# Mixture of experts in a two-layer backbone: 64 slots per expert and unsplit float32 weights in two column halves, instead of 128 slots per group and split weights

## The chip, the cores and the metric

The kernel runs on one core of one Trainium2 chip. The metric is the device time of one execution in microseconds (us), and the kernel before is given by the median of three runs.

## What is computed

The program is a two-layer backbone over 256 latent tokens (with a prefix of 256 context tokens) of 1024 features, all in float32. Layer 0 is an RWKV-7 time mixer, layer 1 a short gated convolution; a mixture of 16 experts follows each of them, and a last norm ends it. The change touches the mixture alone. Of the reference it is this part (d is 1024, EXPERT_DIM 512):

```python
def _moe(h, router_w, router_b, w_gate, w_up, w_down):
    s = sigmoid(hf @ router_w)                         # 256 tokens x 16 experts
    sel = (s + router_b).reshape(-1, 4, 4)             # 4 groups of 4 experts
    group_score = sum(top_k(sel, 2)[0], axis=-1)
    g_idx = argmax(group_score)                        # one group for each token
    experts = g_idx * 4 + top_k(sel[g_idx], 2)         # two experts of this group
    gate = s[experts] / sum(s[experts])
    for e in range(16):
        he = silu(hf @ w_gate[e]) * (hf @ w_up[e])
        out = out + combine[:, e:e + 1] * (he @ w_down[e])
```

Each token takes two experts, so 256 tokens make 512 pairs of a token and an expert, 32 for an expert on average. With the inputs of this reference the fullest group has 84 tokens. In layer 0 no expert has more than 62. In layer 1 one expert, number 15, has 68, and all others have at most 64.

## The kernel before

In both mixtures each expert reads 6 MB of float32 weights: two tables of 1024 x 512 (gate and up) and one of 512 x 1024 (down). SyncE (SP) loads them in pieces of [128, 2048], 1 MB each, in the order of their use, which the generator `sources` (L1045) writes out; `wpiece` (L149) puts each into the next buffer of a ring of 8 (two of the kernel, six of the phase by `extra_ring`, NRING = 6).

A float32 table is not multiplied as it is. ScalarE (ACT) rounds each half piece to the shorter type that the program calls float32r (`wh`, L1078), and VectorE (DVE) subtracts that from the original (`wl`, L1081). The activations are split the same way, and `mm3` (L134) makes each product of three matmuls, high by high, high by low, low by high. `wnext` (L1084) hands out the split parts and `ahead` (L1066) keeps two parts ahead of their use.

The experts of a group share its tokens. `route_groups` (L1341) finds each token's group and its place among the group's tokens. `gather` (L1472) builds a one-hot matrix with 128 slots for each group (`onehot`, L1438) and multiplies the normed tokens with it, for two groups at once: `xe` holds them feature-major. A token that did not choose an expert goes through it all the same and gets the gate weight zero. `route_experts` (L1378) makes the gate weights.

The loop over the experts (L1595) is staggered, and the order of the instructions is the order in which it is written: the gate product of expert e (`half_up`, 8 blocks of 128 features x 3 matmuls of 512 columns), the turn of expert e - 1 (`turn`, `hetp`), the up product of e, and the down product of e - 1 (`down`, 24 matmuls of 512 columns). That makes 72 matmuls of 512 columns for an expert. The down products of the four experts of a group add up in PSUM (`y`), and once per group `scatter` (L1464, 16 matmuls of 256 columns) brings the sum from slots back to tokens. A new group's gate weights come from `gates` (L1450, `gps`).

If a group has more than 128 tokens, `rest` (L1548) computes what is left over. Its body is long (16 experts with weights read again) and stands under one branch for each layer, `tc.If(over > P)`, behind the last expert's turn. With these inputs the branch is never entered. Towards the end of a mixer, two calls `self.ahead(4)` have four parts of the next mixture's weights split beforehand, and the convolution's first weights are split in the same way while the last experts still run. Modulation that is needed late (`fill`, L1091) is computed in the routing, with weights that the caller loads at that point of the program.

## Time and profile before

| | us |
|---|---|
| median of three runs | 1435.24 |
| lowest and highest | 1433.29, 1442.48 |
| profiled execution, span from the first to the last instruction | 1432.6 |
| RWKV mixer, with its output product and the routing of layer 0 | 0 to 680.5 |
| experts of layer 0 | 680.5 to 985.6 |
| convolution mixer and routing of layer 1 | 985.6 to 1119.6 |
| experts of layer 1 | 1119.6 to 1421.0 |
| final norm | 1421.0 to 1432.6 |

The profile is one execution, taken by the hardware's profiler, and its span is the only time that it gives; the stages are cut in the same trace, where the first product of each begins. It is told in the names of the engines: PE is TensorE's matmuls, PEld its weight loads, SP the engine that issues the weights' DMAs. In a timeline the first number is the start in the span, the second the length of a row, and matmuls that follow one another overlap in it, so the cost of one is read from the distance of two starts. The granted clock is a share of full speed.

### The profile page before, as it was taken

To read this page: it belongs to the slowest core of one execution; us is meant where nothing else is said; L and a number is where in the kernel's file an instruction comes from. 1 tells how busy PE (TensorE), PEld (TensorE's weight loads), DVE (VectorE), ACT (ScalarE), POOL (GpSimd) and SP (SyncE) were. 2 spreads that over 40 slices of the span, in tenths; PEclk is the share of its full clock that TensorE was granted. 3 is DMA by queue.
4 is the path that set the end of the run, shared out by engine and by line. 5 is a ranking of instruction groups with operands and counts; after the bars stand their busy time and mean duration, and the time that the engine had idled before them with its cause. 6 is when DMAs were issued, how large, how long until landed. Compare 5 with 4: busy or idle time off the path is not lost. (4 is left out here: it accounts for less than half of the span.)

```text
span 1432.6 us, 23636 instructions
## 1 busy us (share of the span) xinstructions
PE 1289.7 (90%) x8848; PEld 1098.9 (77%) x8848; DVE 1183.9 (83%) x2139; ACT 936.5 (65%) x1499; POOL 235.2 (16%) x245
## 2 busy tenths in 40 slices
PE   2898797998888888998999999997988999999996
PEld 2688696777777777887778787876988778887875
DVE  5869888999989988767888888886685888898985
ACT  4675644676666676445777777765445678777765
POOL 3213525222222312001000000003233000000001
PEclk8899998999999999999999999998999899999998
DMA  9456443223314201386798999986545599999980
GB/s 366 148 170 215 148 141 101 95 91 115 109 32 152 73 25 67 132 319 241 280 348 316 339 349 339 346 322 243 173 154 192 193 354 329 332 344 342 346 292 31
DMA packets 64637, 311.75 MB, mean 218 GB/s; under 512 B 14464, under 2 KB 23040, under 8 KB 29696
## 3 DMA queue, kind: packets, MB, share of 16 engines
q1 hardware_dynamic: 60192, 303.59, 59.2%
q10 hardware_dynamic: 4320, 6.54, 1.3%
q8 instruction: 73, 1.20, 0.3%
q14 instruction: 52, 0.43, 0.1%
HBM read 301.72 MB, written 8.39 MB: 216 GB/s over the span
## 5 line engine op out<-in xcount | busy, mean ns | idle before, releaser
L1081 DVE TENSOR_TENSOR wl<-w,wh 128x1024 fp32r<-128x1024 f32 x411 | 497.6, 1224 | 77.4 <-ACT wh L1078 74.1
L1078 ACT CAST wh<-w 128x1024 fp32r<-128x1024 f32 x424 | 442.0, 1052 | 160.1 <-PE wup L139 69.9
L137 PE MATMUL wup<-wh,xe 128*128 128x512 f32 x512 | 205.4, 401 | 4.3 <-ACT sgate L1602 4.0
L138 PE MATMUL wup<-wl,xe 128*128 128x512 f32 x512 | 202.9, 396 | 0.2
L139 PE MATMUL wup<-wh,xe 128*128 128x512 f32 x512 | 202.3, 395 | 0.0
L137 PEld LDWEIGHTS wup<-wh,xe 128*128 128x128 f32 x512 | 96.1, 188 | 31.6 <-ACT sgate L1602 9.1
L139 PEld LDWEIGHTS wup<-wh,xe 128*128 128x128 f32 x512 | 96.1, 188 | 23.3 <-DVE xe L132 0.3
L138 PEld LDWEIGHTS wup<-wl,xe 128*128 128x128 f32 x512 | 96.2, 188 | 23.1 <-DVE wl L1081 1.6
L137 PE MATMUL y<-wh,het 128*128 128x512 f32 x256 | 102.4, 400 | 8.4 <-PEq L1550 8.4
L138 PE MATMUL y<-wl,het 128*128 128x512 f32 x256 | 102.8, 402 | 0.0
L139 PE MATMUL y<-wh,het 128*128 128x512 f32 x256 | 102.4, 400 | 0.0
L813 DVE TENSOR_TENSOR lv<-a_l,t_l 128x126 f32<-128x126 f32 (+22 forms) x248 | 82.5, 333 | 3.3
L815 DVE TENSOR_TENSOR t_l<-t_l,lv 128x126 f32<-128x126 f32 (+22 forms) x248 | 78.7, 317 | 3.4
L879 PE MATMUL po<-v_bd,hk 128*64 128x128 f32 (+1 forms) x256 | 56.4, 303 | 21.2 <-ACT s_bd L890 8.1
L137 PEld LDWEIGHTS y<-wh,het 128*128 128x128 f32 x256 | 48.9, 191 | 20.6 <-issue 9.2
L879 PEld LDWEIGHTS po<-v_bd,hk 128*64 128x64 f32 (+1 forms) x256 | 31.8, 163 | 41.2 <-ACT s_bd L890 12.8
L1666 POOL TENSOR_SCALAR idrw<-cst 128x1024 f32<-128x1024 f32 x2 | 5.5, 2773 | 343.4 <-PE acc L1469 314.5
L890 ACT COPY s_bd<-po 64x64 f32<-64x64 f32 x112 | 22.6, 204 | 54.6 <-DVE s_bd L889 52.6
L139 PEld LDWEIGHTS y<-wh,het 128*128 128x128 f32 x256 | 48.9, 191 | 11.6
L138 PEld LDWEIGHTS y<-wl,het 128*128 128x128 f32 x256 | 48.9, 191 | 11.3
L138 PE MATMUL dps<-xl,wh 128*128 128x258 f32 x192 | 55.6, 290 | 1.9 <-DVE xl L1271 1.0
L137 PE MATMUL dps<-xh,wh 128*128 128x258 f32 x192 | 55.3, 288 | 1.0 <-ACT rt L1148 1.0
(426 smaller groups left out, 3074.0 us busy)
## 6 DMA issues: line engine op xcount, KB each, us to landing
w<-in_wg SPq DMA_DIRECT2D x64, 1024.0 KB, 5.2
w<-in_wu SPq DMA_DIRECT2D x64, 1024.0 KB, 5.6
w<-in_wd SPq DMA_DIRECT2D x64, 1024.0 KB, 6.0
w<-in_ada SPq DMA_DIRECT2D x46, 1024.0 KB, 6.6
w<-in_sc_in SPq DMA_DIRECT2D x12, 1024.0 KB, 5.5
w<-in_rk SPq DMA_DIRECT2D x8, 1024.0 KB, 5.8
w<-in_wv SPq DMA_DIRECT2D x4, 1024.0 KB, 6.2
w<-in_wo SPq DMA_DIRECT2D x4, 1024.0 KB, 10.5
```

Source lines behind the costliest of these rows:

```text
L137: mm(out, lhs[0], rhs[0], start=start, stop=False)
L138: mm(out, lhs[0], rhs[1], start=False, stop=False)
L139: mm(out, lhs[1], rhs[0], start=False, stop=stop)
L813: nc.vector.tensor_mul(u, a_l[:, kk:kk + 1, kk + 1:].broadcast_to([P, m, n]), t_l[:, 0:m, kk:kk + 1].broadcast_to([P, m, n]))
L815: nc.vector.tensor_sub(t_l[:, 0:m, kk + 1:], t_l[:, 0:m, kk + 1:], u)
L879: nc.tensor.matmul(po[d][i], q.hk[d][g][:, j], q.vbd[:, 4 * g + j], start=True, stop=i == 0)
L890: nc.scalar.copy(sn[64:, 64:], p[0:64, 64:])
L1078: self.nc.scalar.copy(h, w)
L1081: eng.tensor_sub(l, w, h.bitcast(F32))
L1666: nc.gpsimd.tensor_scalar_mul(self.idrw[:, :, :P], kern.k("ident").unsqueeze(1).broadcast_to([P, NB, P]), 1.0)
```

## The change

**Slots.** Every expert gets its own 64 slots (SL = 64). `route` picks the best two experts of every group first, then the group, and numbers the tokens of each expert; `onehot` makes eight matrices of 64 slots for four experts, and `gather` gathers four experts x 64 = 256 columns in one product. `scatter` runs once per expert, not once per group.

**Products.** The weights are used as they are, in float32, one matmul where there were three. Since an expert's activations have only 64 columns, they fill one half of TensorE's columns: the gate product goes to rows 0 to 63 of a PSUM tile and the up product to rows 64 to 127, one after the other in the program, and the two halves of the down product in the same way. The gate weight is applied when the down product leaves PSUM. The scatter takes rows 0 to 63 and 64 to 127 in matmuls of their own (16 of 256 columns).

**The queue of the weights.** Gate and up come in one table, `wgu`, so that an expert takes four pieces `wgu` and two `wd`, in this order and without the stagger. The ring has 2 + 9 = 11 buffers (NRING = 9), and the modulation's weights (`fill`) come through it as well, in the order of `sources`. `pump` issues a load as soon as a buffer is given back by `done`. The splitting stays for the two mixers' own weights, with three buffers instead of four (WSB = 3), which lie in pools of those phases. So `ahead(4)` at the mixers' ends is gone, and the convolution's first weights are split only when its pool is there.

**Overflow.** Experts with more than 64 tokens have a second set of 64 slots, under branches: for each expert from the third on one branch with the gate and up products (`more_up`) and one with the down product and the scatter, both with the weights that are still in the ring; they are given back when the branch is passed (`done(4)`, `done(2)`). The first two experts give their pieces back at once, and have one branch each, which would read the weights again. `over` holds one bit for each expert. `rest` remains for experts with more than 128 tokens. That makes 31 branches for each layer where there was one. With these inputs two of them are entered, those of expert 15 in layer 1.

```diff
-NRING = 6
+NRING = 9
-WSB = 4
+WSB = 3
+SL = 64
+EARLY = 2
...
         def experts(l):
-            for e in range(E + 1):
-                if e < E:
-                    yield from pieces(io["wg"][l, e], io["wu"][l, e])
-                if e:
-                    yield from pieces(io["wd"][l, e - 1])
+            for e in range(E):
+                yield from pieces(io["wgu"][l, e], io["wd"][l, e])
...
+    def pump(self):
+        while len(self.coming) + self.held < self.nring + self.nextra:
+            src = next(self.src, None)
+            if src is None:
+                return
+            self.coming.append(self.wpiece(src))
+
+    def take(self):
+        self.pump()
+        self.held += 1
+        return self.coming.pop(0)
+
+    def done(self, n):
+        self.held -= n
+        self.pump()
...
-            self.ahead(4)
             ro.block(NB - 1)
...
-            def half_up(i, xe):
-                sl = slice(i * P, i * P + P)
+            def gate_up(xe, j, piece, after=lambda k: None):
                 pt = ps.tile([P, 512], F32, tag="m", name="wup")
-                for hf in range(4):
-                    wh, wl = self.wnext(2)
-                    for k in range(2):
-                        kc = hf * 2 + k
-                        self.mm3(pt, (xe[0][:, kc, sl], xe[1][:, kc, sl]), (wh[:, k], wl[:, k]),
-                                 kc == 0, kc == NB - 1)
-                return pt
+                for kc in range(NB):
+                    w = piece(kc)
+                    for i in range(2):
+                        nc.tensor.matmul(pt[SL * i:SL * i + SL], xe[:, kc, j], w[:, 512 * i:512 * i + 512],
+                                         start=kc == 0, stop=kc == NB - 1)
+                    after(kc)
+                sg = pool.tile([SL, FE], F32, tag="sg", name="sgate")
+                nc.scalar.activation(sg, pt[:SL], AF.Silu)
+                nc.vector.tensor_mul(sg, sg, pt[SL:])
+                return sg
...
+            def scatter(yh, yl, st, first=False, last=False):
+                for q in range(4):
+                    for k, y in enumerate((yh, yl)):
+                        for i in range(2):
+                            r = slice(SL * i, SL * i + SL)
+                            nc.tensor.matmul(acc[4 * i + q], y[r, q * P:q * P + P], st[r],
...
+            def many(e):
+                return tc.If((over & (1 << e)) > 0)
+
+            def more_up(e, piece, gw, st, het):
+                g = onehot(e, 1, SL, "go")
+                xe = pool.tile([P, NB, 1, SL], F32, tag="xo", name="xo", bufs=1)
+                for _ in gather(g, 1, xe):
+                    pass
+                gates(g, 0, e, gw, st)
+                turn(gate_up(xe, 0, piece), het)
...
+            for e in range(E):
+                g, xe = gx[e // 4]
+                ws, early = [], e < EARLY
+                sg = gate_up(xe, e % 4, taken(ws), release)
+                gw, st = gate_tiles()
+                gates(g, e % 4, e, gw, st)
+                if out:
+                    scatter(*out)
...
+                if not early:
+                    with many(e):
+                        more_up(e, kept(ws), *og)
+                    self.done(4)
+                wd = []
+                out = (*down(turn(sg, hets()), taken(wd), gw, release), st)
...
+                with many(e):
+                    if early:
+                        more_up(e, again(io["wgu"][l, e]), *og)
+                    scatter(*down(og[2], again(io["wd"][l, e]) if early else kept(wd), og[0]), og[1])
+                if not early:
+                    self.done(2)
+            rest()
```

The scheduler may place instructions of neighbouring steps between one another, so the order in the program is read from the built kernels. On TensorE before, in the middle of a usual expert, the products of the next expert's up table (`wup`), a quarter of the next gather (`xeps`) and the down products (`y`) stand as triples without a break (the numbers in names are buffers):

```order
L137 MATMUL wup<-wh,xe_7452 128x512
L138 MATMUL wup<-wl,xe_7452 128x512
L139 MATMUL wup<-wh,xe_7453 128x512
L1485 MATMUL xeps<-g,h2t_6796 128x256 x2
L1485 MATMUL xeps<-g,h2t_6797 128x256 x2
L1485 MATMUL xeps<-g,h2t_6796 128x256 x2
L1485 MATMUL xeps<-g,h2t_6797 128x256 x2
L137 MATMUL y<-wh,het_8165 128x512
L138 MATMUL y<-wl,het_8165 128x512
L139 MATMUL y<-wh,het_8166 128x512
```

On TensorE after, a usual expert behind its first branch: its own turn, the down products, three products of the next expert, and the compare of the second branch, behind which its body stands (`heto` is the overflow's hidden features):

```order
L1555 MATMUL hetp<-cst,sgate 128x64 x4
L1543 MATMUL wup<-w,xe 64x512
L1568 MATMUL y<-w,het 64x512 x8
L1543 MATMUL wup<-w,xe 64x512 x2
L1696 REGISTER_ALU
L1696 COMPARE_AND_BRANCH
L1568 MATMUL y<-w,heto 64x512 x8
L1582 MATMUL acc_7463<-st,yh 128x256
L1582 MATMUL acc_7464<-st,yh 128x256
```

What moved: a triple has become one matmul of 64 rows, 24 for an expert instead of 72, and TensorE comes to a compare twice in each expert from the third on. On SP before, at the end of layer 0's experts, the loads follow one another, and the one branch stands behind all of the experts' weights:

```order
L158 DMA w<-in_wg 128x2048 x2
L158 DMA w<-in_wu 128x2048 x2
L158 DMA w<-in_wd 128x2048 x4
L1546 TENSOR_LOAD r_cnti
L1550 COMPARE_AND_BRANCH
L1550 UNCONDITIONAL_BRANCH x2
L158 DMA w<-in_sc_in 128x2048
```

On SP after, in the middle of the experts:

```order
L1688 UNCONDITIONAL_BRANCH x2
L161 DMA w<-in_wgu 128x2048 x2
L1696 REGISTER_ALU
L1696 COMPARE_AND_BRANCH
L1696 UNCONDITIONAL_BRANCH x2
L161 DMA w<-in_wgu 128x2048 x2
L161 DMA w<-in_wd 128x2048 x2
L1688 REGISTER_ALU
L1688 COMPARE_AND_BRANCH
```

What moved: the queue of the loads now goes past two branches for each expert, and the pieces are issued two and four at a time behind them.

## Rows read from the trace of the kernel before

**Rows 1.** The page: busy time of the engines.

```profile
PE 1289.7 (90%) x8848; PEld 1098.9 (77%) x8848; DVE 1183.9 (83%) x2139; ACT 936.5 (65%) x1499; POOL 235.2 (16%) x245
```

**Rows 2.** Costliest groups of instructions, from the page.

```profile
L1081 DVE TENSOR_TENSOR wl<-w,wh 128x1024 fp32r<-128x1024 f32 x411 | 497.6, 1224 | 77.4 <-ACT wh L1078 74.1
L1078 ACT CAST wh<-w 128x1024 fp32r<-128x1024 f32 x424 | 442.0, 1052 | 160.1 <-PE wup L139 69.9
```

**Rows 3.** Windows: us, busy PE, PEld, DVE, ACT, POOL, PEclk, DMA share, GB/s.

```profile
630.00:640.00 10.00, 9.81 (x116) 7.91 (x115) 7.11 (x20) 3.36 (x10) 0.61 (x1) 1.00 1.00 423
1160.00:1360.00 200.00, 198.34 (x907) 160.28 (x906) 176.74 (x165) 155.51 (x173) 0.00 (x0) 1.00 0.95 339
680.50:985.60 305.10, 296.34 (x1342) 238.32 (x1345) 260.61 (x247) 226.38 (x249) 0.00 (x0) 0.99 0.90 324
1119.60:1421.00 301.40, 296.03 (x1338) 238.04 (x1337) 258.23 (x245) 225.78 (x250) 0.00 (x0) 0.99 0.84 300
```

**Rows 4.** TensorE's timeline where the experts of layer 0 begin: start us, us.

```profile
680.82 0.39 PE L138 MATMUL wup<-wl,xe 128*128 128x512 f32 x1
681.05 0.40 PE L139 MATMUL wup<-wh,xe 128*128 128x512 f32 x1
```

**Rows 5.** TensorE's timeline before the routing: products of 32 columns of stationary.

```profile
661.11 0.65 PE L179 MATMUL fillps<-w,sc 128*32 128x128 f32 x16
661.68 0.76 PE L1684 MATMUL htps<-idrw,h 128*128 128x144 f32 x4
...
664.42 3.04 PE L179 MATMUL fillps<-w,sc 128*32 128x128 f32 x102
```

**Rows 6.** Groups by form, 560 to 1432 us: busy us, mean ns of one.

```profile
L1611 DVE SCALAR_TENSOR_TENSOR sgate<-sgate,gw,wup 128x512 f32<-128x512 f32 x32 | 23.7, 741 | 1.0 <-PE wup L139 1.0
L1602 ACT ACTIVATE sgate<-wup 128x512 f32<-128x512 f32 x32 | 19.1, 598 | 16.0 <-PE wup L139 16.0
...
L179 PE MATMUL fillps<-w,sc 128*32 128x128 f32 x256 | 8.6, 275 | 0.4 <-ACT rt L1148 0.4
```

**Rows 7.** TensorE's timeline, small products among the experts of layer 0.

```profile
686.19 0.38 PE L1454 MATMUL gps<-cst,g 128*128 128x128 f32 x2
...
687.03 0.50 PE L137 MATMUL wup<-wh,xe 128*128 128x512 f32 x1
...
771.78 0.60 PE L1517 MATMUL hetp<-cst,sgate 128*128 128x128 f32 x4
772.13 0.36 PE L1469 MATMUL acc<-st,yh 128*128 128x256 f32 x1
...
778.33 1.10 PE L1485 MATMUL xeps<-g,h2t 128*128 128x256 f32 x8
779.27 0.28 PE L1469 MATMUL acc<-st,yh 128*128 128x256 f32 x1
...
780.93 0.40 PE L137 MATMUL y<-wh,het 128*128 128x512 f32 x1
```

**Rows 8.** Instructions of the branch, line 1550: duration ns min/median/max.

```profile
L1550 PEldq COMPARE_BRANCH  x2: 3539/4778/6016, 968.5 to 1407.0; - x2
L1550 DVEq COMPARE_BRANCH  x2: 63/68/72, 968.9 to 1408.0; - x2
...
L1550 DVEq EVENT_SEMAPHORE  x2: 21/21/21, 969.5 to 1408.2; - x2
```

**Rows 9.** TensorE's timeline behind the branch, and at the convolution's start.

```profile
974.63 0.76 PE L137 MATMUL y<-wh,het 128*128 128x512 f32 x1 [5.68 <-PEq L1550]
...
986.54 0.39 PE L137 MATMUL dps<-xh,wh 128*128 128x258 f32 x1
```

**Rows 10.** VectorE's timeline in the routing of layer 0.

```profile
667.54 0.16 DVE L1334 TENSOR_REDUCE r_mg<-r_gs 128x2 f32<-128x8 f32 x1
...
667.73 0.17 DVE L1335 TENSOR_TENSOR r_gh<-r_gs,r_mg 128x8 f32<-128x8 f32 x1
```

**Rows 11.** ScalarE's timeline at the start of the convolution mixer.

```profile
992.38 1.99 ACT L1078 CAST wh<-w 128x1024 fp32r<-128x1024 f32 x2
```

More of the change, by code (lines that the diff above doesn't have):

```diff
@@ L1069, in ahead @@
             if not self.loaded:
[L1070 to L1073 removed]
+                t = self.take()
                 self.loaded += [t[:, :1024], t[:, 1024:]]
@@ L1513, in turn, with again, piece, taken @@
-            def turn(sg):
-                pt = ps.tile([P, 4, P], F32, tag="m", name="hetp")
+                    yield
+            def again(src):
+                def piece(k):
+                    w = pool.tile([P, 1024], F32, tag="wov", name="wov")
+                    nc.gpsimd.dma_start(w, src[:, k * 1024:k * 1024 + 1024])
+                    return w
+                return piece
+            def taken(ws):
+                def piece(k):
+                    if k % 2 == 0:
+                        ws.append(self.take())
+                    return ws[-1][:, k % 2 * 1024:k % 2 * 1024 + 1024]
+                return piece
@@ L1516, in turn @@
+            def turn(sg, het):
+                pt = ps.tile([P, 4, SL], F32, tag="m", name="hetp")
                 for k in range(4):
[L1517 to L1539 removed]
@@ new lines, in turn, with hets, down @@
+                    nc.tensor.transpose(pt[:, k], sg[:, k * P:k * P + P], self.k("ident")[:SL, :SL])
+                nc.scalar.copy(het, pt)
+                return het
+            def hets():
+                return pool.tile([P, 4, SL], F32, tag="het", name="het")
+            def down(het, piece, gw, after=lambda k: None):
+                y = psy.tile([P, 512], F32, tag="y", name="y")
+                for k in range(4):
+                    w = piece(k)
+                    for i in range(2):
+                        nc.tensor.matmul(y[SL * i:SL * i + SL], het[:, k], w[:, 512 * i:512 * i + 512],
+                                         start=k == 0, stop=k == 3)
+                    after(k)
+                yh = pool.tile([P, 512], F32R, tag="yh", name="yh")
+                yl = pool.tile([P, 512], F32R, tag="yl", name="yl")
+                nc.scalar.activation(yh, y, AF.Copy, scale=gw)
+                nc.vector.scalar_tensor_tensor(yl, y, gw, yh.bitcast(F32), op0=ALU.mult, op1=ALU.subtract)
+                return yh, yl
@@ new lines, in scatter @@
+            def scatter(yh, yl, st, first=False, last=False):
+                for q in range(4):
+                    for k, y in enumerate((yh, yl)):
+                        for i in range(2):
+                            r = slice(SL * i, SL * i + SL)
+                            nc.tensor.matmul(acc[4 * i + q], y[r, q * P:q * P + P], st[r],
+                                             start=first and q % 2 + k == 0, stop=last and k == 1,
+                                             skip_group_check=True)
@@ L1594, in moe @@
[L1594 to L1616 removed]
+                                nc.tensor.transpose(pt[:, k], sgs[t][:, k * P:k * P + P], self.k("ident"))
@@ new lines, in group @@
+            def group(e0, turns):
+                g = onehot(e0, 4, 0, "g")
+                xe = pool.tile([P, NB, 4, SL], F32, tag="xe", name="xe")
+                gx.append((g, xe))
+                yield from gather(g, 4, xe, 2, turns)
+            gx = []
+            for _ in group(0, (psy, ps)):
+                pass
+            cmb = self.weights(one, s, o)
+            ci = self.counts(one, o)
+            over, most = [nc.values_load(ci[0:1, i:i + 1], min_val=0, max_val=m,
+                                         skip_runtime_bounds_check_because=why)
+                          for i, (m, why) in enumerate((((1 << E) - 1, "one bit for each of the experts"),
+                                                        (T, "a count of the T tokens")))]
@@ L1619, in moe @@
                     out = None
-                if mid is not None:
-                    if e % 4 == 1:
-                        y = [psy.tile([P, 512], F32, tag="y", name="y") for _ in range(2)]
-                        yst = st
-                    out = down(het, y, e % 4 == 1, e % 4 == 0, yst if e == E else None)
-                    out = (*out, yst) if out[0] is not None else None
-                mid = nxt
-            scatter(*out, False, True, range(NB // 2, NB))
+                if e % 4 == 0 and e + 4 < E:
+                    nxt = group(e + 4, (psy, psy))
@@ new lines, in moe @@
+                if nxt and next(nxt, 0) == 0:
+                    nxt = None
+                og = (*gate_tiles("o"), pool.tile([P, 4, SL], F32, tag="heto", name="heto", bufs=1))
+                if not early:
[4 more added lines that the diff above has]
+                out = (*down(turn(sg, hets()), taken(wd), gw, release), st)
+                if e == 0:
+                    scatter(*out, first=True)
+                    out = None
```

378 lines of the change are left out of this document (167 added, 211 removed).

## The prediction, made before the changed kernel ran

> **What bounds the kernel now.** I read the page's busy times first: TensorE has 90% of the span and VectorE 83% [rows 1]. The second number comes from the splitting: 411 subtractions of 1.22 us make 497.6 us, and ScalarE's 424 roundings 442.0 us [rows 2]. That looks like two engines at the limit, so the windows must decide [rows 3]. The two stretches of the experts last 305.1 and 301.4 us, and TensorE is busy for 296.3 and 296.0 of them; in the 200 us window inside layer 1's stage it is busy for 198.3, VectorE for 176.7, ScalarE for 155.5. TensorE bounds the experts. The copies do not: they run at 339 GB/s there, though their engines show a share of 0.95, and the same queue moved 423 GB/s from 630 to 640 us, where it had a backlog. In the experts the products stand 0.23 us apart (681.05 - 680.82) [rows 4], so the 72 products of an expert take 72 x 0.233 = 16.8 of the 19.07 us that an expert has (305.1 / 16; in layer 1 301.4 / 16 = 18.84).
>
> So the question is what one expert costs TensorE after the change. I call it p.
>
> **The products.** An expert has 24 float32 products of 512 columns, each with 64 columns of stationary. The nearest thing in the trace is the modulation's `fillps`: unsplit float32, 128 columns moving, 32 columns of stationary, four quarters in turn. Its 64 products stand as 128 records, two for a product, 118 of them in [rows 5]. 102 of these take 3.04 us; less the 0.275 us that the last one lasts (mean in [rows 6]), 101 distances make 2.765 us, 27.4 ns each, and four quarters 109.5 ns. This is what one product of 256 columns of the shorter type takes (14 of them between 779.27 and 780.93, 0.119 each [rows 7]). I read two things there: a float32 record streams its columns twice, and the four quarters run abreast. A record of 512 columns then takes 4 x 109.5 = 438 ns, two halves abreast 219 ns each, and the expert's 48 records 10.5 us. If the halves ran one after the other it would be 21.0; I take 10.5, since quarters that did not overlap could not stand 27.4 ns apart. The matmuls of a pair that meet a new piece or another tile start alone: I add 0.4 (0 to 0.8).
>
> **The small products.** The gate weights (`gps`) come once per expert instead of once per four: 687.03 - 686.19 = 0.84 [rows 7]. The gather: eight `xeps` in 779.27 - 778.33 = 0.94, now eight per expert. The turn (`hetp`): 772.13 - 771.78 = 0.35. The scatter, 16 products of 256 columns for each expert: 16 x 0.119 = 1.9 one after another, 0.95 if the row halves run abreast. No row shows row halves; I take 1.2.
>
> **Changes between halves and whole.** In [rows 5] 16 records from 661.11 end their issue at 661.11 + 16 x 0.0274 = 661.55, and the next, whole product starts at 661.68: 0.13 lost. Five such changes in an expert make 0.6 (0 to 1.2). The Trainium skill ("TensorEngine Tiling (Array Packing)", Key Properties) says that changing the tiling mode drains TensorE; 0.13 is smaller than the 0.275 that a record lasts, so by a full drain it would be 5 x 0.275 = 1.4 and the sum 0.8 x 32 = 26 us higher, an estimate.
>
> **The branches.** From the third expert on, each has two. The row of before has only a branch over a very long body: TensorE's compare lasted 3.5 and 6.0 us [rows 8], and TensorE stood idle for 5.68 us in layer 0 [rows 9]. VectorE, over a body of the same branch but with fewer instructions, needed 0.07 us for the compare, and its next event came 0.6 and 0.2 us later. The new bodies are short on TensorE (some 56 products and 24). I take 0.5 for each branch, between VectorE's lower 0.2 and twice its upper 0.6, nearest to VectorE's rows; hence 1.0 for an expert. What is queued behind: `hetp`, whose activations have long been ready, and the next products. For the wait on `het` behind ScalarE's copy, under which only one product stands, I add 0.2 (0 to 0.6).
>
> p = 10.5 + 0.4 + 0.84 + 0.94 + 0.35 + 1.2 + 0.6 + 1.0 + 0.2 = 16.0 us. All upper ends make 18.9. The lower ends make less than the copies allow: six pieces of 1.049 MB at 423 GB/s [rows 3] are 14.9 us, which is the lower bound that I use. A ring of 11 pieces, with some given back late, should keep that backlog, so TensorE remains the bound, narrowly. What covers the loads is that backlog: SP's queue now goes past two branches for each expert, and a piece whose buffer is given back behind one may be asked for late. Without cover, one late piece would cost 1.049 / 423, 2.5 us. The splitting that goes, 12 roundings and 12 subtractions of half pieces for an expert, wins nothing by itself, since it lay beside TensorE.
>
> **The stages.** Layer 0: 16 x 16.0 = 256.0, plus the first expert's scatter, which cannot hide its copies (1.5), plus the branch over `rest`, still long (mean of 3.5 and 6.0, 4.8): 262.3, that is 42.8 less than 305.1. Layer 1 enters the two bodies of expert 15, the last one. Gather 32 x 0.119 = 3.8, `gps` 0.84, 32 records 7.0, turn 0.35, 16 records 3.5, scatter 1.2, and two chains through ScalarE and VectorE with nothing beside them, 1.3 each (by the activation and the product at the gates of before, 0.598 + 0.741 [rows 6]): 19.3. The stage is then 281.6, 19.8 less than 301.4.
>
> **The rest of the program.** The routing has 20 short VectorE steps ahead of the ranks where it had 10. A step takes 667.73 - 667.54 = 0.19 [rows 10], but in before other steps stood between them, so I take 1 us for each layer (0 to 3). The convolution's first weights are no longer split in advance. ScalarE's first cast in that mixer stands at 992.38 [rows 11], behind the activations, where TensorE had begun at 986.54 [rows 9]; with 1.05 and 1.22 for the first cast and subtraction [rows 2], TensorE could begin 8 us later. Part of it returns, as TensorE then finds parts waiting: 5 (0 to 8).
>
> Sum: -42.8 - 19.8 + 2 + 5 = -55.6. The profiled span of 1432.6 becomes 1377.0; the median of the runs is 2.6 above that span, so 1380 us. One microsecond of p is worth 32 us; the change gains nothing at p = 17.7.
>
> **The rivals.** *The copies set the pace.* If the small costs lie at their lower ends, p falls to 14.9: 1.1 x 32 = 35 less, 1345 us. For it: most of my small terms are bounds rather than rows. Against it: the pieces are given back in fours and twos behind branches, which costs backlog.
>
> *The gain is eaten on TensorE.* Branches at 1.2 us add 1.4 to p, 1425 us; the scatter's row halves one after another add 0.7 more, 1447. For it: no row shows either. Against it: VectorE's 0.2 to 0.6.
>
> *Every branch costs like the one of before.* This is the way to the slower side. There are 60 branches besides `rest`. At 3.5 us, the lower of the two that TensorE showed, they cost 60 x 3.0 = 180 more, 1560 us; at 6.0, 1710. It decides from 0.5 + 55.6 / 60 = 1.4 us per branch. For it: the only rows on TensorE. Against it: the body jumped there holds the products of 16 experts, the new ones a part of one. The Trainium skill ("Runtime: NRT & Kernel Launch", Instruction fetch mechanics) says that a taken branch whose target lies outside the current two pages of instructions must fetch them first; by it the new short jumps stay cheap, and only `rest` pays.
>
> *The halves do not run abreast.* Then p is 10.5 higher, 336 us, 1716. Against it stands [rows 5]; for it, only that those were quarters, of 32 columns each.
>
> **How the numbers follow.** A measurement of this kernel can tell about 1% from no change. Forecast (p from 15.3 to 17.2, 1358 to 1418): 0.57. Copies: 0.17. Gain eaten (1425 to 1447): 0.13. Branches dear: 0.09; halves in turn: 0.04. The first two are faster by over 1% (below 1421), 0.74; the third is within 1% for the most part, 0.13; the last two slower, 0.13. The range goes from below the copies' case, 1338, to the end of the third case, 1448.
>
> **What would show it.** Starts of `wup` records 0.22 us apart in the middle of an expert; a `MATMUL` group of 16 `acc` of 1.0 to 1.9 us; TensorE's compares at lines 1688 and 1696 under 0.6 us, except in expert 15 of layer 1; the rate of the copies near 390 GB/s in the experts; a gap of some 5 us at the start of the convolution. Starts 0.44 us apart, idle time of several microseconds put down to TensorE's queue at these two lines, or TensorE waiting for `w` in most experts would make the prediction wrong.

## The result: slower by 1.7%, and the profile after

The changed kernel takes 1460.5 us (median of five runs, 1459.43 to 1471.34) against 1438.8 us for the kernel before (five runs): a ratio of 1.0169, with an interval of 1.0142 to 1.0195. Forecast were 1380 us, with 1338 to 1448 as the range. The profiled execution is the longest of the five, 1471.34 us, with a span of 1469.3; a second profile has 1465.8, and its first stage of experts is the same to 0.1 us. This is where its time went, stage by stage, against the working of the prediction (each stage ends where TensorE begins the next):

| stage | before | foretold | after |
|---|---|---|---|
| mixer of layer 0, to the first `fillps` | 660.1 | 660.1 | 672.4 |
| routing of layer 0 | 20.4 | 21.4 | 22.6 |
| experts of layer 0 | 305.1 | 262.3 | 296.6 |
| convolution mixer | 116.4 | 121.4 | 120.9 |
| routing of layer 1 | 17.7 | 18.7 | 18.9 |
| experts of layer 1 | 301.4 | 281.6 | 324.6 |
| rest | 11.6 | 11.6 | 13.3 |

The span is 92.3 us over the 1377.0 of the working, and 34.3 + 43.0 of that lie in the two stages of the experts, 12.3 in the first mixer. The other rows are within 2 us. The page after, the busy times and the largest groups (to be held against [rows 1] and [rows 2]):

```profile
PE 1235.0 (84%) x8842; PEld 863.7 (59%) x8842; DVE 740.9 (50%) x1823; ACT 561.0 (38%) x1155; POOL 234.4 (16%) x245
...
L1543 PE MATMUL wup<-w,xe 128*64 128x512 f32 x1024 | 258.5, 617 | 4.1 <-PEq L1696 2.0
...
L1568 PE MATMUL y<-w,het 128*64 128x512 f32 x512 | 141.4, 690 | 11.2 <-ACT het L1556 11.2
L1574 DVE SCALAR_TENSOR_TENSOR yl<-y,gw,yh 128x512 fp32r<-128x512 f32 x33 | 24.8, 751 | 200.0 <-ACTq L1696 182.0
```

No engine is at its limit any more. VectorE has fallen from 83% to 50%, as the splitting went, and TensorE from 90% to 84%. The windows of the two stages (columns as in [rows 3]) say the same of the copies:

```profile
695.00:991.60 296.60, 247.53 (x1272) 107.26 (x1271) 35.40 (x77) 38.68 (x76) 0.00 (x0) 0.95 0.86 341
844.00:880.00 36.00, 30.46 (x150) 12.76 (x152) 3.22 (x7) 4.27 (x9) 0.00 (x0) 0.91 0.86 348
1131.40:1456.00 324.60, 276.73 (x1378) 120.42 (x1377) 38.95 (x87) 43.49 (x85) 0.00 (x0) 0.92 0.70 276
```

In layer 0's stage TensorE is idle for 296.6 - 247.5 = 49.1 us, 3.1 for each expert, where before it was idle for 8.8; the granted clock is 0.95; the copies run at 341 GB/s, far from 423. The instructions of the first branch of each expert are these:

```profile
L1688 PEldq COMPARE_BRANCH  x29: 77/325/422, 736.6 to 1439.8; - x29
...
L1688 DVEq COMPARE_BRANCH  x29: 47/56/63, 739.3 to 1439.0; - x29
```

The jump itself is cheap: 0.33 us on TensorE's queue, 0.06 on VectorE's, both in the median. What costs is seen in TensorE's largest waits of the stage (us in total, times, longest; L1688 is the first branch of an expert, L1696 the second, L1605 the one over `rest`):

```profile
PE hetp L1555 <- DVEq L1688: 21.1, 14, 1.6
PE acc L1582 <- ACTq L1696: 7.1, 9, 0.8
PE acc L1582 <- PEq L1605: 6.8, 1, 6.8
PE y L1568 <- ACT het L1556: 5.6, 12, 0.5
PE gps L1488 <- DVEq L1696: 4.4, 8, 0.6
```

How the first of them comes about is shown by all engines' timeline around one branch (start us, us, engine):

```profile
841.78 1.03 PE L1543 MATMUL wup<-w,xe 128*64 128x512 f32 x4
842.85 0.59 ACT L1547 ACTIVATE sgate<-wup 64x512 f32<-64x512 f32 x1 [3.03 <-PE wup L1543]
...
843.48 0.69 DVE L1548 TENSOR_TENSOR sgate<-sgate,wup 64x512 f32<-64x512 f32 x1 [3.07 <-ACTq L1688]
...
844.37 0.43 PE L1555 MATMUL hetp<-cst,sgate 64*128 64x64 f32 x4 [1.56 <-DVEq L1688]
844.84 0.37 ACT L1556 COPY het<-hetp 128x256 f32<-128x256 f32 x1 [1.40 <-PE hetp L1555]
...
845.26 1.07 PE L1568 MATMUL y<-w,het 128*64 128x512 f32 x2 [0.46 <-ACT het L1556]
```

TensorE's last `wup` ends at 842.8. Then ScalarE's activation (0.59) and VectorE's product (0.69) run one after the other with nothing beside them, the branch is passed on each engine in turn (the releasers are ACTq and DVEq of L1688, the queues' branch instructions), and TensorE starts its turn 1.56 us later and waits 0.46 more for the copy. The first pair of its down products then lasts 1.07 us where 0.64 is usual (the pair at 848.68, once the clock is back). TensorE's own timeline shows what that comes to, 16 records of each kind:

```profile
839.15 3.65 PE L1543 MATMUL wup<-w,xe 128*64 128x512 f32 x16
...
845.26 5.35 PE L1568 MATMUL y<-w,het 128*64 128x512 f32 x16 [0.46 <-ACT het L1556]
```

The same work takes 5.35 us behind the waits and 3.65 ahead of them. The granted clock of the stretch behind the waits (columns as above) is 0.51, the lower of its two levels (1.2 of 2.4 GHz), after 2.5 us in which TensorE did nothing but the turn:

```profile
845.26:848.68 3.42, 3.42 (x8) 0.96 (x10) 0.00 (x0) 0.00 (x0) 0.00 (x0) 0.51 0.99 417
```

### The profile page after: what moved, and what is told of

Read it like the earlier page. It is cut to its first block, busy times and chain, and to the rows that moved or that the text cites. A ratio compares the mean times of both kernels' runs of the same rounds, so it can differ in the third digit from the quotient of the medians.

```text
span 1469.3 us, 23339 instructions
## 1 busy us (share of the span) xinstructions
PE 1235.0 (84%) x8842; PEld 863.7 (59%) x8842; DVE 740.9 (50%) x1823; ACT 561.0 (38%) x1155; POOL 234.4 (16%) x245
## 5 line engine op out<-in xcount | busy, mean ns | idle before, releaser
L1543 PE MATMUL wup<-w,xe 128*64 128x512 f32 x1024 | 258.5, 617 | 4.1 <-PEq L1696 2.0
L1543 PEld LDWEIGHTS wup<-w,xe 128*64 128x64 f32 x1024 | 76.6, 139 | 126.5 <-issue 118.5
L1568 PE MATMUL y<-w,het 128*64 128x512 f32 x512 | 141.4, 690 | 11.2 <-ACT het L1556 11.2
L1574 DVE SCALAR_TENSOR_TENSOR yl<-y,gw,yh 128x512 fp32r<-128x512 f32 x33 | 24.8, 751 | 200.0 <-ACTq L1696 182.0
L1548 DVE TENSOR_TENSOR sgate<-sgate,wup 64x512 f32<-64x512 f32 x33 | 22.8, 690 | 192.0 <-ACT sgate L1547 100.5
L1547 ACT ACTIVATE sgate<-wup 64x512 f32<-64x512 f32 x33 | 19.5, 590 | 200.1 <-PE wup L1543 200.1
L1568 PEld LDWEIGHTS y<-w,het 128*64 128x64 f32 x512 | 44.7, 155 | 85.3 <-issue 68.4
L884 PE MATMUL po<-v_bd,hk 128*64 128x128 f32 (+1 forms) x256 | 56.6, 304 | 20.8 <-ACT s_bd L895 7.5
L1582 PE MATMUL acc<-st,yh 64*128 64x256 f32 x264 | 45.9, 314 | 26.6 <-ACTq L1696 14.2
L1102 ACT CAST wh<-w 128x1024 fp32r<-128x1024 f32 x40 | 41.6, 1046 | 48.3 <-PE dps L141 32.3
L1582 PEld LDWEIGHTS acc<-st,yh 64*128 64x128 f32 x264 | 29.8, 193 | 46.7 <-ACTq L1696 30.2
L142 PE MATMUL dps<-xh,wl 128*128 128x258 f32 x192 | 55.7, 290 | 0.6 <-POOL wl L1105 0.6
```

The source lines that it names most:

```text
L142: mm(out, lhs[1], rhs[0], start=False, stop=stop)
L884: nc.tensor.matmul(po[d][i], q.hk[d][g][:, j], q.vbd[:, 4 * g + j], start=True, stop=i == 0)
L1102: self.nc.scalar.copy(h, w)
L1543: nc.tensor.matmul(pt[SL * i:SL * i + SL], xe[:, kc, j], w[:, 512 * i:512 * i + 512], start=kc == 0, stop=kc == NB - 1)
L1548: nc.vector.tensor_mul(sg, sg, pt[SL:])
L1568: nc.tensor.matmul(y[SL * i:SL * i + SL], het[:, k], w[:, 512 * i:512 * i + 512], start=k == 0, stop=k == 3)
```

## The experiments

Theory A: the branches. An engine passes one only when it has finished all that stands ahead of it, and what uses a tile that the body could have touched waits for the other engines' passing too. Theory B: the lost stagger. In the kernel before, the turn of expert e - 1 stood behind a product of expert e, so the activation had time; now the activation that the turn needs comes from the product just ahead of it.

**Without branches (e1).** With no branch to keep them for, the pieces of all experts are given back at once.

```diff
-EARLY = 2
+EARLY = E
...
-                if not early:
-                    with many(e):
-                        more_up(e, kept(ws), *og)
-                    self.done(4)
...
-                with many(e):
-                    if early:
-                        more_up(e, again(io["wgu"][l, e]), *og)
-                    scatter(*down(og[2], again(io["wd"][l, e]) if early else kept(wd), og[0]), og[1])
-                if not early:
-                    self.done(2)
```

> The changed kernel without the 30 branches of each layer and their bodies; it leaves out the second 64 slots (4 tokens of expert 15 in layer 1). In the changed kernel's trace TensorE is idle for 49 and 48 us in the two stages, about 3 us per expert. Theory A (each branch is a point where an engine must have finished all that is ahead of it): idle falls to under 1 us per expert and the granted clock returns to 1.0, p from 18.3 to about 15.4; 2 x 16 x 2.9 = 93 less, and 20 less for the bodies of expert 15, from 1460 to about 1350 us. Theory B (the chain from the last gate and up product through ScalarE and VectorE to the turn is bare because the loop has lost its stagger): only the waits at line 1696 go, about 1.3 us per expert, 42 + 20 less, about 1400 us, and the wait ahead of hetp stays near 1.5 us.

Measured: 1372.37 us, ratio 0.9525 (0.9482 to 0.9567), between the two. Layer 0's stage:

```profile
694.80:958.40 263.60, 235.33 (x1272) 107.48 (x1271) 36.54 (x80) 38.22 (x76) 0.00 (x0) 0.99 0.98 382
```

That is 33.0 us shorter, so the stage's 30 branches cost 1.1 us each. Of the 33.0, 20.8 are idle time and 12.2 busy time, at a granted clock of 0.99 where it was 0.95; 3.8 of the idle time are the jump over `rest`, 3.0 here against 6.8, which the edit does not touch. That the pieces come back earlier has no large part in it: in the changed kernel's stage no wait of TensorE is put down to a load, and 0.5 us ahead of `wup` to nothing that the profile names. But 28 us of idle time stay, and most of it is the bare chain (waits of TensorE, 736 to 930 us; total, times, longest):

```profile
PE hetp L1555 <- DVE sgate L1548: 11.3, 8, 1.4
PE y L1568 <- ACT het L1556: 5.2, 10, 0.5
```

So both theories hold a part.

**One branch for each expert (e2).** Both bodies in one branch, behind the down products.

```diff
-                if not early:
-                    with many(e):
-                        more_up(e, kept(ws), *og)
-                    self.done(4)
...
                 with many(e):
-                    if early:
-                        more_up(e, again(io["wgu"][l, e]), *og)
+                    more_up(e, again(io["wgu"][l, e]) if early else kept(ws), *og)
                     scatter(*down(og[2], again(io["wd"][l, e]) if early else kept(wd), og[0]), og[1])
                 if not early:
-                    self.done(2)
+                    self.done(6)
```

> One branch for each expert instead of two, behind the down products, with gate and up, down and scatter in its body; all six pieces are kept until it is passed. Theory A: half of the joins go; with some 1.5 us each and the clock, 45 less, about 1415 us. Theory B: the chain ahead of hetp stays, within 10 us of 1460. If the ring of 11 is short with six pieces held, TensorE waits for w and the time is above 1460.

Measured: 1445.82 us, ratio 1.0053 (1.0030 to 1.0076): 15 less than the changed kernel, between the two expectations again. Layer 0's stage lasts 287.3 us, with 16 branches where there were 30. A removed branch saved (296.6 - 287.3) / 14 = 0.66 us, less than half of what theory A said. The wait ahead of the turn stayed without the branch, now put down to the product that it needs, and the wait at the remaining branch grew from 7.1 us to 11.0 (waits of TensorE in the stage):

```profile
PE hetp L1555 <- DVE sgate L1548: 13.4, 10, 1.4
PE acc L1582 <- ACTq L1692: 11.0, 14, 0.8
```

**The stagger back, the branches kept (e3).** The gate and up products of e + 1 stand ahead of the branch of e.

```diff
-                yield from pieces(io["wgu"][l, e], io["wd"][l, e])
+                if e < E:
+                    yield from pieces(io["wgu"][l, e])
+                if e:
+                    yield from pieces(io["wd"][l, e - 1])
...
+                    sg = gate_up(xe, e % 4, taken(ws), release)
...
+                if mid:
+                    f, fsg, fws, fgw, fst = mid
...
+                        with many(f):
+                            more_up(f, kept(fws), *og)
```

> Both branches of each expert stay, but the gate and up products of expert e + 1 stand ahead of the first branch, the turn and the down products of expert e (the pieces come in the order wgu(e + 1), wd(e)). Theory A: the joins stay, within 15 us of 1460. Theory B: the 1.56 us ahead of hetp goes in all experts from the third on, and with it half of the clock's loss: 2 x 14 x 1.9 = 53 less, about 1405 us.

Measured: 1473.97 us, ratio 1.0244 (1.0212 to 1.0276). Theory B alone would have given 1405; the wait was as long as ever (waits, 736 to 930 us):

```profile
PE hetp L1558 <- DVEq L1700: 14.9, 10, 1.6
PE acc L1585 <- ACTq L1708: 6.7, 8, 0.8
```

The data for the turn was old, but the releaser is the branch on VectorE's queue. The timeline shows that this engine came to the branch only behind the activation of e + 1, which hangs on the newest product:

```profile
809.48 0.59 ACT L1550 ACTIVATE sgate<-wup 64x512 f32<-64x512 f32 x1 [3.03 <-PE wup L1546]
...
810.10 0.69 DVE L1551 TENSOR_TENSOR sgate<-sgate,wup 64x512 f32<-64x512 f32 x1 [3.07 <-ACTq L1700]
...
810.99 0.43 PE L1558 MATMUL hetp<-cst,sgate 64*128 64x64 f32 x4 [1.56 <-DVEq L1700]
```

The theory that followed: a branch binds the turn to the youngest work that stands ahead of it on any engine, needed or not.

**The activation behind the first branch (e11).** The same kernel, with `gated`, the activation of e + 1, at the end of the step. Two things went with it: the bodies take their PSUM tiles from the other pool (in e3 they go through the same two buffers as `hetp`), and the gate weights and the gather of e + 1 stand behind the turn, no longer ahead of the branch.

```diff
-                    sg = gate_up(xe, e % 4, taken(ws), release)
-                    gw, st = gate_tiles()
-                    gates(g, e % 4, e, gw, st)
+                    up = gate_up_mm(xe, e % 4, taken(ws), release)
...
+                    het = turn(fsg, hets())
+                if e < E:
+                    gw, st = gate_tiles()
+                    gates(g, e % 4, e, gw, st)
...
-                mid = (e, sg, ws, gw, st) if e < E else None
+                mid = (e, gated(up), ws, gw, st) if e < E else None
```

> The staggered run e3 once more, with both branches of each expert and the pieces kept, and one thing else: the activation of expert e + 1 (ScalarE, VectorE) stands behind the branches of e, no longer ahead of them, with the PSUM tiles of the bodies taken from the y pool so that this is possible. In e3 TensorE still waited 20 us of a stage ahead of hetp. If that was because the joins on ScalarE and VectorE stand behind the youngest activation, the wait ahead of hetp falls from 20 us to under 6, the stage of layer 0 from 305 to 275 or less, and the time from 1474 to about 1410 us. If a join costs its 1.5 us whatever stands ahead of it, the stage stays above 295 and the time at 1460 or more.

Measured: 1393.79 us, ratio 0.9691 (0.9662 to 0.9719), 80 us less than e3, with the same branches in the same number and the whole computation kept. It beats both kernels. Layer 0's stage, in e3 and here, and TensorE's timeline around a turn here:

```profile
695.00:1000.50 305.50, 251.89 (x1272) 106.17 (x1271) 35.47 (x77) 38.55 (x76) 0.00 (x0) 0.94 0.80 318
692.50:954.90 262.40, 243.50 (x1272) 100.33 (x1271) 35.30 (x77) 38.55 (x76) 0.00 (x0) 1.00 0.92 374
```

```profile
817.10 0.39 PE L1589 MATMUL acc<-st,yl 64*128 64x256 f32 x2
817.33 0.41 PE L1562 MATMUL hetp<-cst,sgate 64*128 64x64 f32 x4
817.66 0.44 PE L1491 MATMUL gps<-cst,g 128*128 128x128 f32 x2
```

The turn follows without a gap; of the waits ahead of `hetp` 0.3 us are left in the stage, where e3 had 19.6, and the granted clock is 1.00. The 6.6 us for which e3's TensorE waited on the copy `het` are gone too, since the gate weights and the gather now stand there.

So the order around the branches is worth 43 us of a stage, but the run does not tell its three parts apart. One row speaks for the shared tiles as a condition. In the built kernel the activation stands between the two branches of e, just ahead of the second one (L1716), and there it costs nearly nothing:

```profile
806.41 0.59 ACT L1554 ACTIVATE sgate<-wup 64x512 f32<-64x512 f32 x1 [1.31 <-PE wup L1547]
...
807.04 0.69 DVE L1555 TENSOR_TENSOR sgate<-sgate,wup 64x512 f32<-64x512 f32 x1 [1.36 <-ACTq L1716]
...
808.24 1.94 PE L1575 MATMUL y<-w,het 128*64 128x512 f32 x8 [0.16 <-PEq L1716]
```

TensorE goes on with the second half of the down products, into a tile already begun and with data long there, and waits 0.16 us. Whether e3 with the other pool alone would have been as fast was not tried.

**What the branch costs where nothing young stands ahead of it.** e7 adds 30 branches to the kernel before, whose schedule has little idle time (8.8 us in layer 0's stage).

```diff
                 if e == E:
                     rest()
+                elif e:
+                    with tc.If(over > P):
+                        gates(g, grp % 2, grp, "o")
```

> The kernel before with one more branch in each expert from the second on (15 for each layer), behind the turn, never entered, whose body is one call of gates on tiles of its own. It measures the price of a branch in a schedule that is staggered and has no idle time. The prediction's price is 0.5 us: 15 us more, ratio 1.01. Theory A (a join that passes from engine to engine, some 1.5 us, and the clock behind it): 30 x 1.5 to 2.5, 45 to 75 more, ratio 1.03 to 1.05.

Measured: 1453.37 us, ratio 1.0107 (1.0072 to 1.0143). The stages of the experts grew from 305.1 to 314.8 and from 301.4 to 307.2, 15.5 us for 30 branches, 0.52 each: the price of the prediction.

```profile
683.30:998.10 314.80, 298.24 (x1341) 239.12 (x1341) 260.73 (x246) 227.91 (x249) 0.00 (x0) 0.98 0.87 314
1130.40:1437.60 307.20, 295.12 (x1337) 236.72 (x1337) 258.33 (x245) 227.39 (x250) 0.00 (x0) 1.00 0.82 295
```

e9 and e10 measure it in a staggered version of the changed kernel with the activation late, as in e11, with one branch for each expert (both bodies, weights read again) and without any; e10 leaves out the second 64 slots. Both also give all pieces back at once and ask for wo early (the edit of e6, below).

```diff
+                    if f:
...
+                        for j in (0, 1) if f == 1 else (f,):
+                            with many(j):
+                                more_up(j, again(io["wgu"][l, j]), *og)
+                                scatter(*down(og[2], again(io["wd"][l, j]), og[0], side="o"), og[1])
+                    het = turn(fsg, hets())
...
+                    out = (*down(het, taken([]), fgw, release), fst)
+                mid = (e, gated(up), gw, st) if e < E else None
```

> A version that keeps the whole computation. One branch for each expert, one step late: the order is gate and up products of e + 1, scatter of e - 1, the branch of e (both bodies, weights read again, PSUM tiles of the y pool), then the turn of e, gate weights, gather, the down products of e, and only then the activation of e + 1 on ScalarE and VectorE. So at the branch ScalarE and VectorE have nothing young ahead of them, and what TensorE does next does not wait for the join. The first pieces of wo come early as in the run before. If a branch by itself costs 0.5 us (0.53 in the kernel before with 30 branches), idle time is about 0.6 us per expert, p about 16.1, layer 0's stage 260 us, layer 1's 290 with expert 15's bodies, and the time about 1385 us, ratio 0.965. If each join still brings its 1.5 us, p is 17.1 and the time about 1420. If the jump itself is dear as in the run with 16 branches in a row (2.8 us), the time is 1460 or more.

> The same without the branches and their bodies; it leaves out the second 64 slots (4 tokens of expert 15 in layer 1). It gives the stage without joins and without the bare chain: idle time under 0.5 us per expert; the weights' copies at 418 GB/s then are the bound, p = 15.0 to 15.7, layer 0's stage 240 to 252 us, about 1335 to 1350 us in all. The difference of layer 0's stages to the run above, over 15 branches, is the price of a branch: 0.5 to 0.7 us by the cheap reading, 1.5 by theory A.

Measured: e9 1408.06 us, ratio 0.9811 (0.9776 to 0.9847); e10 1326.98 us, ratio 0.9231 (0.9200 to 0.9262). Layer 0's stage takes 251.7 and 241.5: 10.2 us for 16 branches, 0.64 each. e9's median is 23 us above the expectation; its profiled execution, 1395, has 251.7 for layer 0's stage (260 expected) and 299.7 for layer 1's (290). Layer 0's stage of e9 and of e10:

```profile
687.40:939.10 251.70, 230.79 (x1273) 97.53 (x1272) 35.26 (x77) 38.69 (x76) 0.00 (x0) 0.99 0.99 399
693.30:934.80 241.50, 229.34 (x1273) 99.15 (x1271) 34.85 (x78) 37.98 (x76) 0.00 (x0) 1.00 1.00 411
```

In e10 the copies run at 411 GB/s, and they and TensorE (229.3 of 241.5) are near their limits together. e12 keeps the last expert's six pieces for its branch:

```diff
-                    up = gate_up_mm(xe, e % 4, taken([]), release)
+                    up = gate_up_mm(xe, e % 4, taken(ws), release if e < E - 1 else lambda k: None)
...
-                                more_up(j, again(io["wgu"][l, j]), *og)
...
+                                more_up(j, kept(ws) if last else again(io["wgu"][l, j]), *og)
```

> The version e9 with the last expert's six pieces kept for its branch, which then stands behind its down products, instead of read again. In e9 layer 1's stage was 48 us longer than layer 0's (299.7 against 251.7), for bodies that the changed kernel did in 20 us with kept pieces. If the reading again is what made the difference, layer 1's stage falls by 20 to 25 us and the time from 1408 to about 1385, ratio 0.965; layer 0's stage stays within 3 us of 252. If not, the time stays above 1400.

Measured: 1400.55 us, ratio 0.9718 (0.9664 to 0.9772), where 1385 was expected. Layer 1's stage is 284.6, 15 less. 11.2 of that can be read in e9's trace, as TensorE's waits for the weights that are read again (`wov`), which e12 does not have:

```profile
PE wup L1549 <- DMA wov<-in_wgu: 7.7, 6, 2.5
PE y L1577 <- DMA wov<-in_wd: 3.5, 2, 2.6
```

A fall of 20 to 25 was expected. Layer 1's stage is now 18 above layer 0's, where it had been 48, but half of that change comes from layer 0's stage: it is 266.5, 15 more than in e9, which the edit doesn't explain. The two traces differ there by 7.7 us of busy time (granted clock 0.96 against 0.99), 3.6 at the jump over `rest` and 4.2 of waits at `gps` with no releaser named; e9's own six runs went from 1395 to 1413. Why is left open.

**All branches at one place (e5), and wo's place on SP (e6).** e5 is staggered, and the branches of all 16 experts stand in a row behind the last one's gate and up products.

```diff
+                    if f == E - 1:
...
+                        for j in range(E):
+                            with many(j):
+                                more_up(j, again(io["wgu"][l, j]), *og)
+                                scatter(*down(og[2], again(io["wd"][l, j]), og[0]), og[1])
```

> Staggered as in the run before, but all 16 branches of a layer stand one behind the other at one place, behind the gate and up products of the last expert, with both bodies in one and the weights read again; the pieces are given back at once. The whole computation is kept. If the joins are what made the stagger useless, TensorE's idle time per expert falls below 0.6 us (the run without branches had 1.6, most of it the bare chain ahead of hetp), the stage of layer 0 lasts 16 x 15.1 + 16 joins of 0.6 = 252 us against 296 in the changed kernel and 264 in the run without branches, and layer 1, with the bodies and their reading again, about 290; about 1385 us in all. If the stagger is of no use even without joins between, layer 0's stage stays at 264 + 10 and the time near 1405.

Measured: 1469.48 us, ratio 1.0209 (1.0175 to 1.0243): a miss for both readings. Up to the row of branches the stage was as hoped; then TensorE stood still (windows, then the branch instructions):

```profile
735.00:775.00 40.00, 38.29 (x228) 21.38 (x226) 7.50 (x20) 7.11 (x15) 0.00 (x0) 1.00 1.01 419
935.00:965.00 30.00, 0.00 (x0) 0.00 (x0) 0.00 (x0) 0.00 (x0) 0.00 (x0) 0.50 0.08 30
```

```profile
L1701 PEldq COMPARE_BRANCH  x33: 77/2723/5539, 929.0 to 1447.7; - x33
```

The same branches in e9, over the same body, with an expert's work between two of them:

```profile
L1696 PEldq COMPARE_BRANCH  x33: 77/337/3905, 713.4 to 1370.3; - x33
```

The median is 0.34 us there and 2.7 here, where jump followed jump; TensorE was idle for 44.5 us in one piece.

e6 is e5 with the first pieces of wo asked for ahead of `h`:

```diff
+            self.nw = -1
+            self.pump()
             ro.begin()
```

> The same, and the ring's count is set so that its two early buffers go to the first two pieces of wo, asked for ahead of the stream x (h), as in the kernel before, where now two pieces of modulation had them and wo stood behind h on SP. If the place on SP is why the first product with wo came at 632.9 instead of 619.2, it comes 8 us sooner than in the run above and the time falls by 6 to 8 us. If not (the products wait for the scan that runs beside them), nothing changes, within 2 us.

Measured: 1472.59 us, ratio 1.0242 (1.0210 to 1.0274), no gain over e5's 1469.48. In its profile the first product with wo did come early (8.9 us behind the last `pq<-gq`, a product of the mixer's scan; 14.9 in the changed kernel), but `fillps` came 54.1 behind it, against 54.4. The time is lost further on, where TensorE waits for the last pair's own result. In the changed kernel's timeline of TensorE:

```profile
662.78 0.41 PE L930 MATMUL pyt<-cst,yt 128*128 128x128 f32 x2 [2.65 <-DVE yt L926]
...
664.79 0.58 PE L1035 MATMUL oacc<-h2t,wh 128*128 128x256 f32 x1 [1.14 <-ACT h2t L134]
```

**The two controls.** Both kernels once more.

> The changed kernel once more, for a second profile: its profiled execution was the slowest of its five. Whether the 5.7 us that the RWKV mixer is behind the kernel before at its last scan (618.0 against 611.7 and later) belong to the change: if so, they are there again; if they are scatter of one execution, the span is about 1458 and the mixer's scan ends near 612. The first product with wo comes some 8 us late in either case.

> The kernel before once more, for a second profile. The RWKV mixer's last pq<-gq product stood at 611.7 us, and at 618.0, 617.9, 615.7, 616.5 and 613.4 in five profiles of the changed kernel and its variants, whose mixer has the same instructions. If this is scatter, it comes between 611 and 618 here too; if it stays near 611.7, some 4 us belong to the change.

Measured: spans of 1465.8 and 1437.4. The last `pq<-gq` starts at 617.9 and 616.1, where it had started at 618.0 and 611.7. So two executions of the kernel before differ by 4.4 us there, and of the 6.3 by which the changed kernel was late the controls leave 1.9. From there to `fillps` the kernel before takes 48.4 us in both profiles, the changed one 54.4 in both: 6 us belong to the change.

## Why the prediction was wrong

**The products: right.** Sixteen `wup` records take 3.65 us in the changed kernel's timeline, 0.59 of that the last one's own length. They start in pairs, as their weight loads show:

```profile
840.06 0.14 PEld L1543 LDWEIGHTS wup<-w,xe 128*64 128x64 f32 x2 [0.29 <-issue]
840.49 0.14 PEld L1543 LDWEIGHTS wup<-w,xe 128*64 128x64 f32 x2 [0.29 <-issue]
```

From pair to pair it is (3.65 - 0.59) / 7 = 0.437 us, 0.219 for a record, as foretold. The halves run abreast. A pair of the scatter's halves costs 0.12 (starts at 835.16, 835.27 and 835.39 in the same timeline), so 0.95 for an expert, the lower of the bounds (1.2 was taken). p without branches and without the wait on `het` was 14.8, which with the 6.3 us at the ends makes 243 for layer 0's stage; e10 measured 241.5. The rival of the halves in turn is out, and that of the copies came true only where nothing else was in the way (e10).

**The step that failed** is the one on the branches, and in it the sentence on what is queued behind: "`hetp`, whose activations have long been ready". They were not. In the changed program the turn follows the very product whose activation it needs. Between the product and the turn stand ScalarE's 0.59 and VectorE's 0.69 us. The kernel before had a product of another expert there; the diff shows the loop without that stagger, and the working priced its loss at 0.2 us for `het`. The runs give: e1 against e10, 263.6 - 241.5 = 22.1 us for a stage, 1.4 for an expert.

**The price of a branch was a property of its place.** The second term that was too small is the 0.5 us for a branch. It was right where no engine had young work ahead that the next product waits for (0.52 in e7, 0.64 in e9). In the changed kernel it was (296.6 - 263.6) / 30 = 1.1; with the order of e11 the same 30 branches cost (262.4 - 241.5) / 30 = 0.70. Foretold for a stage were 3.2 for the stagger and 16 for the branches; measured 22.1 and 33.0. The difference, 35.9, is the miss of layer 0, with 1.6 us on the other side from the products. The split depends on the order in which the two are taken out: with the branches left in, the stagger alone (e3) won nothing. Of the 55.1 us of both, 36.9 are idle time and 18.2 are busy time: TensorE was busy for 247.5 us in the changed kernel and for 229.3 in e10, with the same products. The lower granted clock (0.95 against 1.00) is a part of the 18.2 and not all, since e11 was busy for 243.5 us at 1.00. The working had no term for more busy time.

The second rival, the gain eaten on TensorE, had 1.2 us for a branch, near the 1.1 measured, but left the stagger at 0.2; with a dearer scatter it ended at 1447. The third, that every branch costs like the one of before, is out: TensorE's compares took 0.33 and 0.23 us in the median, and only the one over `rest` several. The prediction's upper ends, added up again, make 19.5 us for an expert (0.8, 0.84, 0.94, 0.35, 1.9, 1.2, 2.4 and 0.6 on top of 10.5), not 18.9. The stage had (296.6 - 1.5 - 6.8) / 16 = 18.0, so the single bounds held in their sum; the range, which ended with the second rival, did not use them.

**Layer 1** has 8.7 us more of a miss: with the bodies of expert 15 its stage took 324.6 - 296.6 = 28.0 us more than layer 0's, against 19.3. It varies from one execution to the next: in the second profile it is 24.6 (321.1 - 296.5). From 1419 to 1456 us the granted clock is 0.82. In e11, at 0.99, the difference is 281.7 - 262.4 = 19.3, as foretold:

```profile
1095.00:1376.70 281.70, 262.94 (x1378) 110.65 (x1377) 38.85 (x87) 42.16 (x84) 0.00 (x0) 0.99 0.79 318
```

**The first mixer** was priced at nothing. 6 of its 12.3 us belong to the change (the controls), and the waits of 2.65 and 1.14 us for the last pair's result lie in them; the kernel before has none at this place. The other 6.3 are for the most part scatter: the last `pq<-gq` starts at 611.7, 613.6 and 616.1 in the three profiles with the mixer of before (e7 is the third), and from 613.4 to 618.0 in e1, e2, e3, e5, e11 and the two of the changed kernel, which have the mixer of after. What put the wait of 2.65 us there was not tried further; that wo's loads stand behind `h` on SP is not it (e6).

**The rest was right**: the convolution's start cost 4.5 (5 foretold), the routing 2.2 and 1.2 (1 each), `rest` 6.8 and 3.2 of idle time (4.8 foretold).

## What to carry to other kernels

A branch whose body is never entered costs little for its jump and can cost much for what it binds together: ask which instruction stands last ahead of it on every engine, and whether what follows on the busiest engine uses a tile that the body shares. Move young work behind the branch, and give the body tiles of its own; e11 did both at once. Before you take a stagger out of a loop, write down the chain from a product to its next use, with the durations of the row; if nothing stands beside it, that is the price for each step. An engine's gain is worth only what the waits between engines leave of it: TensorE's busy time fell by 55 us over the whole span, and the time rose.

## What the runs showed of the hardware that was not expected

Jumps in a row are dear on TensorE's queue, 2.7 us in the median (e5), and the same jumps spread out are not, 0.34 (e9). The Trainium skill ("Runtime: NRT & Kernel Launch", Instruction fetch mechanics) says that instructions are fetched ahead in sequence and that a taken branch to outside the current two pages must wait for the fetch; these two runs agree with it, if the fetch catches up during an expert's work, which no run here shows. The prediction had used that rule for the opposite, that short jumps stay cheap.

The granted clock does not follow idle time alone. Layer 0's stage had 49 us of idle time at 0.95 in both profiles of the changed kernel, and 48 at 0.98 in e2. What decides there was not tried.
